# A hybrid decoder layer on one core: first loads in one queue, nine idle matmuls on ones, first products by token pairs, first sums in their own step, stores of row factors and states in longer runs

## The chip, the core and the metric

The kernel runs on one core of one Trainium2 chip. Its engines work beside each other, each through its own instructions in order: TensorE (PE) multiplies, VectorE (DVE), ScalarE (ACT) and GpSimd (POOL) work on tiles, and SyncE (SP) issues DMAs, as ACT and POOL also do. The metric is the device time of one execution in microseconds; lower is better.

## The reference

One inference step of one layer: 4096 prompt tokens and 64 sample tokens of width 1024 are normalised, multiplied by one large matrix, and the result is shared out among three head groups (a gated short convolution, windowed attention with sinks, attention to memory), whose outputs go through a second matrix.

```python
def _layer(x, conv_buf, buf_k, buf_v, mem_k, mem_v, g_pre, g_post, w_in, conv_w, sink, w_out, prompt):
    h = _rmsnorm(x, g_pre)
    z = h @ w_in
    cb, cc, ch, cg, q, k, v, ag, mq, mg = _split_cols(z)
    u = cc * ch
    up = jnp.concatenate([conv_buf, u], axis=1)
    conv = conv_w[0] * up[:, 0:t] + conv_w[1] * up[:, 1:t + 1] + conv_w[2] * up[:, 2:t + 2]
    out_a = jax.nn.silu(cg) * cb * conv
    ...
    y = jnp.concatenate([out_a, out_b, out_c], axis=-1) @ w_out
    return x + _rmsnorm(y, g_post), new_conv, new_k, new_v
```

Besides the two outputs, the last convolution inputs (`conv_prompt`, `conv_sample`), the new keys and values and the memory's keys and values are returned.

## The kernel before

**Tiles.** The 4160 tokens are cut into eight blocks (`NBLK`) of 520, each of two halves of 260 (`HW`). Tokens lie along the free dimension, the 1024 channels on 128 partitions by eight (`KT`). The input product z = h @ w_in is done in three phases, one per set of output columns (`PHASES`); phases 0 and 1 hold four pairs of 128 columns, q = 0 to 3, phase 2 three. A float32 product is made of three matmuls per 128 channels: value and weight are each split into a rounded part (`hi`) and the rest (`lo`), and hi x hi, hi x lo and lo x hi are added. ACT makes `hi` by a copy, DVE makes `lo` by a subtraction (`split` L383, `x_split` L608, `w_split` L214). One such product of 4 x 128 channels is 12 matmuls of 128x260 (`product` L392).

**Steps.** From block 2 of phase 0 on, each block takes seven steps p = 0 to 6 (`PRODUCTS`) of products with sums of quarter matrices in Winograd's way, instead of eight: of x the parts B11, B21, B12, B22 and the sums T1 = B12 - B11, T2 = B22 - T1, T3 = B22 - B12, T4 = B21 - T2 (`t_sum`, L367, DVE). Blocks 0 and 1 of phase 0 are done plainly in eight steps s = 0 to 7 (`plain_block` L697), since the sums of the weights (S1 to S4) aren't there yet. A step is four products, q = 0 to 3, 48 matmuls. The steps of the next block prepare its x: load, gain by channel (ACT), factor by token (DVE), T1, and the split of the step to come. With `high_first`, the eight matmuls with `hi` of x come ahead of the four with `lo`; before, this holds for q = 0 of steps 0 and 2 of phase 0 and for a few steps of phases 1 and 2 (`HIGH_FIRST`).

**Row factors.** 1 / rms of every token is computed from x in natural order: tiles `nat` of 104 tokens, five to a block, are squared and summed on ACT (`row_step` L300), POOL takes the power, and the 104x5 factors are stored to `rowd` in device memory (L321), from which they are loaded again, spread over all partitions (`rows_load` L282), when the block's x is scaled. `row_queue` (L341), called once in each step, counts the steps between store and load in `row_spreads`. For blocks 0 and 2 the factors also go through PE (`rows_diag`, `rows_product`).

**Order.** In phases 0 and 2 the five engines' instructions stand as the code is written (`written_order` L721); in phase 1 a scheduler places them, save those in `keep`. Each engine takes its own in order, so a wait holds what is behind it. SP issues nearly all loads in the same way; the stores of phase 0 go out from POOL (`store` L198).

**The start** (L726 to L745). The first half of x in two parts, and weight tiles of 128x512, `wr_qA21` for product q, are loaded: x and tiles 2, 3 from SP, tiles 0, 1 from ACT. Meanwhile PE works seven idle matmuls on `ones` and `ident`. The first step has the matmuls of a product in the order hi x hi for the four k, hi x lo for the four, lo x hi for the four (`opening`).

**Conv states.** `finish_conv` (L475) of block 0 stores the samples' last inputs from a tile of 8x10 (`o_convs`), that of the last block the prompt's (`o_convp`), both in phase 1.

Of the kernel before, what the change touches and what calls it, by code (L numbers as in the profile page):

```python
# [8 lines left out]
F32 = mybir.dt.float32  # L9
# [6 lines left out]
P = 128  # L16
# [36 lines left out]
def hybrid_layer(ctx: ExitStack, tc: tile.TileContext, a: dict):  # L53
# [31 lines left out]
    make_identity(nc, ident)  # L85
# [7 lines left out]
    zs = const.tile([P, 14, NS], F32, name="zs")  # L93

# [167 lines left out]
    def x_load(ph, b, o, parts=KH):  # L262
# [37 lines left out]
    def row_step():  # L300
# [13 lines left out]
        if i == 4:  # L314
            G.tensor_scalar(r[:RG, 0:5], r[:RG, 0:5], 1.0 / D, EPS, op0=ALU.mult, op1=ALU.add)
            G.tensor_tensor(r[:RG, 0:5], r[:RG, 0:5], mhalf[:RG, 0:5], op=ALU.pow)
# [4 lines left out]
            G.dma_start(rowd[b].rearrange("(i p) -> p i", p=RG), r[:RG, 0:5])  # L321
            if b > 0:
                row_spreads[b] = 4
# [17 lines left out]
    def row_queue():  # L341
# [4 lines left out]
        for b in [b for b, n in row_spreads.items() if n == 1]:  # L346
            rows_load(b)
# [44 lines left out]
    def product(w, h, bank, first=True, last=True, opening=False, high_first=False):  # L392
        order = [(l, r, k) for l, r in ((0, 0), (0, 1), (1, 0)) for k in range(KH)] if opening else \
# [68 lines left out]
    ub_prev, us_of = [None, None], []  # L462
# [12 lines left out]
    def finish_conv(b, ct, zc, zh, zg, zb):  # L475
# [6 lines left out]
        if ns:  # L482
# [4 lines left out]
            store(a["o_convs"][ct], us[:, :, 8:10])  # L487
# [5 lines left out]
        if b == NBLK - 1:  # L493
            store(a["o_convp"][ct], ub_prev[ct])
# [62 lines left out]
    def x_of(ph, b, o, parts=KH):  # L557
        if ph == 0 or b < PLAIN_BLOCKS:
            t = x_load(ph, b, o, parts)
# [17 lines left out]
    def next_block(ph, b, p):  # L577
# [19 lines left out]
        if nph < 2:  # L597
            if p == 6:
# [9 lines left out]
    def x_split(b, o):  # L608
        x = xs[0, b][o]
        h0[b, o] = hi, lo = [h_tile(n, f"{n}0_{b}{o}") for n in ("hi", "lo")]  # L610
        for k in range(KH):
# [40 lines left out]
    def plain_jobs(b, s):  # L652
# [16 lines left out]
            (0, 6): lambda: [*parts(1, "B11"), *row, *fills(1, "S1", "S4"), *sums(3, 0), *row],  # L669
            (0, 7): lambda: [*row, *fills(3, "S2", "S3"), lambda: rows_diag()],  # L670
# [65 lines left out]
    for _ in range(7):  # L736
        TE.matmul(idle[:, 0, :P], ones, ident, start=True, stop=True)
    w = ws[0, 0, "A21"] = w_slot(0, "w0_0A21")
    V.tensor_copy(w[:, 0], raw0[0, "A21"])
    x_split(0, "B11")  # L740
    V.tensor_tensor(w[:, 1], raw0.pop((0, "A21")), f(w[:, 0]), op=ALU.subtract)
# [251 lines left out]
    def input_projection():  # L993
        for i, (ph, b, p) in enumerate(steps):
# [66 lines left out]
            for q in quads:  # L1061
# [5 lines left out]
                product(ws[ph, q, PRODUCTS[p][0]], hs[i], acc[:, q % 2], high_first=q == 0 and (p in (0, 2) if ph == 0 else (ph, b, p) in HIGH_FIRST))  # L1067
# [10 lines left out]
            if p >= 5:  # L1078
# [4 lines left out]
                elif ph == 1 and b == 0:  # L1083
                    when = (1, *(2,) * len(ends))
# [804 lines left out]
```

## Time and profile before

| | us |
|---|---|
| median of 3 runs | 1456.57 |
| lowest and highest run | 1455.95, 1457.87 |
| the profiled execution | 1455.13 |
| its span in the trace | 1453.4 |
| start of the first product; of the second step | 5.77; 13.53 |
| start of step (2, 0) of phase 0 | 100.57 |
| start of block 1 of phase 1 | 380.45 |
| end of the last matmul | 1447.15 |

The profile is one execution, and all durations are from it. A row of a timeline has the start, the duration of the merged instructions, engine, line, operation, tiles (written <- read, without the buffers' numbers) and the count; in brackets stands how long the engine had been idle before, and who ended that. PE is busy in all stages, so where PE waits and how late it starts is what can be won; an idle time of another engine counts only where PE waits behind it. The page's chain of waits runs 82% of the span along PE, 8% along DMAs, 4% along DVE.

### The profile page before, as it was taken

To read this page: it belongs to the slowest core of one execution; us is meant where nothing else is said; L and a number is where in the kernel's file an instruction comes from. 1 tells how busy PE (TensorE), PEld (TensorE's weight loads), DVE (VectorE), ACT (ScalarE), POOL (GpSimd) and SP (SyncE) were. 2 spreads that over 40 slices of the span, in tenths; PEclk is the share of its full clock that TensorE was granted. 3 is DMA by queue.
4 is the path that set the end of the run, shared out by engine and by line. 5 is a ranking of instruction groups with operands and counts; after the bars stand their busy time and mean duration, and the time that the engine had idled before them with its cause. 6 is when DMAs were issued, how large, how long until landed. Compare 5 with 4: busy or idle time off the path is not lost.

```text
span 1453.4 us, 30932 instructions
## 1 busy us (share of the span) xinstructions
PE 1442.0 (99%) x11453; PEld 1324.3 (91%) x11453; DVE 1206.5 (83%) x1899; ACT 756.0 (52%) x1868; POOL 447.1 (31%) x622
## 2 busy tenths in 40 slices
PE   9999999999999999999999999999999999999998
PEld 9999999999999999999999999978777787777777
DVE  6879888899998877799678778998998889888853
ACT  6776665566522222234445534656566555655641
POOL 0223323212300000000002224275665566556661
PEclk9999999999999999999999999999999999999999
DMA  9999999896866644475987978999988899998773
GB/s 266 160 275 232 293 269 277 238 307 215 226 223 198 192 136 150 140 273 143 323 276 228 290 231 266 324 261 238 238 217 224 215 258 228 238 237 223 233 220 105
DMA packets 212124, 337.27 MB, mean 232 GB/s; under 512 B 55301, under 2 KB 126213, under 8 KB 211941
## 3 DMA queue, kind: packets, MB, share of 16 engines
q1 hardware_dynamic: 159189, 226.29, 52.7%
q0 software_dynamic: 44144, 78.68, 21.3%
q10 hardware_dynamic: 8640, 30.33, 6.7%
q8 instruction: 91, 1.49, 0.5%
q14 instruction: 60, 0.49, 0.1%
HBM read 192.48 MB, written 110.15 MB: 208 GB/s over the span
## 4 chain that ended last, share of the span: by engine, by line
PE 82%; DMA 8%; DVE 4%; issue 3%; ACT 2%; SPq 1%; POOL 1%; POOLq 0%; ACTq 0%; DVEq 0%
PE c L397 46%; PE y L1675 24%; PE pv L1144 5%; PE ws L1144 3%; DMA place<-in_xt 2%; PE xs L1144 2%; DMA nat<-in_x_p 2%; DMA wr_3A<-in_w_in 1%; PE mem_acc L825 1%; DMA md<-th 1%; DVE z L649 1%; DMA x_1B<-in_xt 1%; DMA vd<-v 1%; DMA wr_3S<-sd6S 1%; DMA w<-s 0%
## 5 line engine op out<-in xcount | busy, mean ns | idle before, releaser
L1675 PE MATMUL y<-wo,mh 128*128 128x512 f32 (+1 forms) x1040 | 328.7, 391 | 0.0
L403 DVE TENSOR_TENSOR z<-c,z 128x520 f32<-128x520 f32 (+1 forms) x308 | 193.6, 644 | 61.3 <-PE c L397 60.5
L1675 PEld LDWEIGHTS y<-wo,mh 128*128 128x128 f32 x1040 | 194.2, 188 | 52.4 <-DVE wmx L1303 5.4
L1675 PE MATMUL y<-wo,ml 128*128 128x512 f32 (+1 forms) x520 | 201.0, 387 | 0.0
L1347 POOL TENSOR_SCALAR s<-s,x 128x256 f32<-128x256 f32 x124 | 58.0, 480 | 199.1 <-DVE x L1342 193.5
L1675 PEld LDWEIGHTS y<-wo,ml 128*128 128x128 f32 x520 | 97.8, 188 | 18.5
L1313 ACT ACTIVATE s<-s,wnm 128x128 f32<-128x128 f32 x256 | 98.7, 387 | 0.0
L771 POOL MEMSET negs<- 128x1 f32 x1 | 0.1, 100 | 281.7 <-DVE w_2A L219 281.7
L1290 ACT COPY s<-ws 128x256 f32<-128x256 f32 x128 | 41.3, 378 | 77.4 <-PE ws L1144 68.5
L1705 POOL TENSOR_TENSOR xr<-yn,xr 128x1024 f32<-128x1024 f32 x29 | 69.3, 2390 | 18.4 <-ACT yn L1704 17.7
L1378 POOL TENSOR_SCALAR_AFFINE_SELECT wd<-w 128x512 f32<-128x512 f32 x64 | 60.2, 941 | 38.2 <-DMA w<-s 21.7
L1683 ACT ACTIVATE y<-y 128x512 f32<-128x512 f32 (+1 forms) x66 | 38.6, 585 | 52.8 <-DVE yn L1682 52.7
L1336 ACT ACTIVATE s<-xs,x 128x256 f32<-128x256 f32 x128 | 58.1, 461 | 0.0
L1682 DVE TENSOR_TENSOR yn<-y,gpost 128x512 f32<-128x512 f32 (+1 forms) x66 | 44.7, 677 | 16.0 <-PE y L1675 14.5
L1144 PEld LDWEIGHTS ws<-kst,q 64*128 64x128 f32 x768 | 47.7, 185 | 11.0 <-issue 9.5
L1378 POOL TENSOR_SCALAR_AFFINE_SELECT w<-w 128x512 f32<-128x512 f32 x64 | 55.5, 887 | 2.2
L1144 PE MATMUL ws<-kst,q 64*128 64x256 f32 x768 | 55.0, 288 | 0.0
L1294 DVE COPY_PREDICATED s<-wmask,ws 128x256 f32<-128x256 uint8 x124 | 48.0, 441 | 8.0 <-ACT s L1290 6.0
L309 ACT ACTIVATE nat<-nat 104x1024 f32<-104x1024 f32 x40 | 42.3, 1058 | 19.2 <-DMA nat<-in_x_p 19.2
L405 ACT COPY z<-c 128x520 f32<-128x520 f32 (+1 forms) x44 | 24.1, 553 | 53.0 <-PE c L397 50.0
L1313 ACT ACTIVATION_READ_ACCUMULATOR s<-s,wnm 128x1 f32 x256 | 47.9, 187 | 0.0
L200 POOL DMA_DIRECT2D md<-th x48 | 26.2, 547 | 66.9 <-DVE th L457 40.3
(970 smaller groups left out, 4805.6 us busy)
## 6 DMA issues: line engine op xcount, KB each, us to landing
w<-s SPq DMA_DIRECT2D x456, 64.0 KB
q<-qd POOLq DMA_DIRECT2D x32, 768.0 KB, 6.6
xr<-in_x_p SPq DMA_DIRECT2D x32, 512.0 KB
nat<-in_x_p SPq DMA_DIRECT2D x39, 416.0 KB
o_yp<-xr SPq DMA_DIRECT2D x31, 512.0 KB
md<-th POOLq DMA_DIRECT2D x48, 260.0 KB, 7.0
qd<-zh SPq DMA_DIRECT2D x48, 260.0 KB
qd<-z SPq DMA_DIRECT2D x48, 260.0 KB
```

What stands on the lines that cost most here:

```text
L309: S.activation(t[:RG], t[:RG], AF.Square, accum_out=r[:RG, i : i + 1])
L397: TE.matmul(bank[:, :HW], w[:, l, k * P : (k + 1) * P], h[r][:, k], start=first and i == 0, stop=last and i == 3 * KH - 1)
L403: add = lambda dst, other: V.tensor_tensor(dst, c, other, op=ALU.add)
L1144: ins = TE.matmul(o, w, x, **kw)
L1294: V.copy_predicated(to, squares(third["wmask"]), squares(s3[:, :, 0:P]))
L1313: S.activation(sm[:, h], sm[:, h], AF.Exp, bias=nm[:, h : h + 1], scale=SCALE, accum_out=den[:, h : h + 1])
L1336: S.activation(p[:, i], s[:, i].rearrange("p (a k j) -> p a k j", a=2, k=4), AF.Exp, bias=nm[:, i : i + 1], scale=SCALE, accum_out=den[:, ...
L1347: G.tensor_scalar(p[:, i], p[:, i], rd[:, i : i + 1], 0.5, op0=ALU.mult, op1=ALU.mult)
L1378: G.affine_select(out, src, pattern=[[32 * sign, 2], [0, 8], [sign, 32]], compare_op=op, fill=0.0, base=base * sign, channel_multiplier=-s ...
L1675: TE.matmul(acc, self.hl[l][:, k], wo[k][c0 // 512][:, r, c0 % 512 : c0 % 512 + c1 - c0], start=j == 0, stop=j == passes * KT - 1)
L1682: V.tensor_tensor(yn[:m, c0:c1], acc[:m], gpost[0][:m, c0:c1], op=ALU.mult)
L1705: total = G.tensor_tensor(self.xr, yn, self.xr, op=ALU.add)
```

## The change

The first loads all go out from SP, x's second part after weight tile 0 (`between`), and weight tile 0 is split like the others, its `hi` now by ACT. The nine idle matmuls use `ones` twice, and `ones` is filled before `ident`. `opening` goes by pairs of k. The row factors are turned on DVE (a 32x32 transpose of `turned`, a part of `zs`), so that the store writes runs of 32 or 8 floats instead of single ones, two `row_queue` calls later than before; `rows_diag` comes a step earlier. T1 of a block is summed in the block's own step 0, ahead of T2 in the list of jobs there, not in step 6 of the block before. `high_first` holds for q = 0 of every step of phase 0. In phase 1 the splits of steps 0 and 1 of block 0 are kept in place, and block 0's second conv finish moves from two steps later to three. `o_convs` is packed by POOL ahead of its store, and `o_convp` is stored in phase 2.

```diff
     ones = const.tile([P, P], F32, name="ones")
     G.memset(ones, 1.0)
+    make_identity(nc, ident)
...
+    turned = zs[:, 10, 0:32]
+    G.memset(turned, 0.0)
...
             for k in range(0, KH, parts):
+                if k:
+                    between()
                 DMA.dma_start(t[:, k : k + parts, g - g0 : g - g0 + w], src[:, KH * kh + k : KH * kh + k + parts, off : off + w])
...
-            G.dma_start(rowd[b].rearrange("(i p) -> p i", p=RG), r[:RG, 0:5])
-            if b > 0:
-                row_spreads[b] = 4
+            G.tensor_copy(turned[:RG, 0:5], r[:RG, 0:5])
+            row_spreads[b] = 4
...
-        for b in [b for b, n in row_spreads.items() if n == 1]:
+        for b in [b for b, n in row_spreads.items() if n == 3]:
+            V.transpose(turned, turned)
+            for g in range(0, RG, 32):
+                n = min(32, RG - g)
+                G.dma_start(rowd[b].rearrange("(i p) -> i p", p=RG)[:, g : g + n], turned[g : g + 5, :n])
+        for b in [b for b, n in row_spreads.items() if n == 1 and b > 0]:
             rows_load(b)
...
-        order = [(l, r, k) for l, r in ((0, 0), (0, 1), (1, 0)) for k in range(KH)] if opening else \
+        order = [(l, r, k + n) for k in (0, 2) for l, r, n in ((0, 0, 0), (0, 1, 0), (0, 0, 1), (1, 0, 0), (0, 1, 1), (1, 0, 1))] if opening else \
...
-            store(a["o_convs"][ct], us[:, :, 8:10])
+            last = tiny.tile([P, 16], F32, tag="x4", name=f"convs{ct}")
+            G.tensor_copy(last.rearrange("p (b t) -> p b t", b=NB), us[:, :, 8:10])
+            store(a["o_convs"][ct].rearrange("p b t -> p (b t)"), last)
...
-            store(a["o_convp"][ct], ub_prev[ct])
+            convp.append(lambda: store(a["o_convp"][ct], ub_prev[ct]))
...
-            hs[i] = split(xs[ph, b][o], f"{ph}_{b}{o}", (ph, b) == (1, 1) and p < 2)
+            hs[i] = split(xs[ph, b][o], f"{ph}_{b}{o}", (ph, b) in ((1, 0), (1, 1)) and p < 2)
...
-            if p == 6:
+            if (nph, nb, p) == (1, 0, 6):
                 jobs.append(lambda: t_sum(nph, nb, "T1"))
...
-            (0, 6): lambda: [*parts(1, "B11"), *row, *fills(1, "S1", "S4"), *sums(3, 0), *row],
-            (0, 7): lambda: [*row, *fills(3, "S2", "S3"), lambda: rows_diag()],
+            (0, 6): lambda: [*parts(1, "B11"), lambda: rows_diag(), *row, *fills(1, "S1", "S4"), *sums(3, 0), *row],
+            (0, 7): lambda: [*row, *fills(3, "S2", "S3")],
...
-    x_of(0, 0, "B11", 2)
-    first_w("A21", 0, queue=S)
     S.mul(tiny.tile([P, 16], F32, tag="x4", name="table")[:, :8], mhalf, 1.0)
-    first_w("A21", 1, queue=S)
-    first_w("A21", 2, 3)
+    x_of(0, 0, "B11", 2, lambda: first_w("A21", 0))
+    first_w("A21", 1, 2, 3)
...
-    for _ in range(7):
-        TE.matmul(idle[:, 0, :P], ones, ident, start=True, stop=True)
-    w = ws[0, 0, "A21"] = w_slot(0, "w0_0A21")
-    V.tensor_copy(w[:, 0], raw0[0, "A21"])
-    x_split(0, "B11")
-    V.tensor_tensor(w[:, 1], raw0.pop((0, "A21")), f(w[:, 0]), op=ALU.subtract)
+    for _ in range(9):
+        TE.matmul(idle[:, 0, :P], ones, ones, start=True, stop=True)
+    x_split(0, "B11", 0)
+    first_fill("A21", 0)
+    x_split(0, "B11", 1, 2, 3)
...
+            if ph < 2 and p == 0 and i and (ph, b) != (1, 0):
+                jobs.insert(0, lambda: t_sum(ph, b, "T1"))
...
+            if (ph, b, p) == (2, 3, 0):
+                jobs += convp
...
-                product(ws[ph, q, PRODUCTS[p][0]], hs[i], acc[:, q % 2], high_first=q == 0 and (p in (0, 2) if ph == 0 else (ph, b, p) in HIGH_FIRST))
+                product(ws[ph, q, PRODUCTS[p][0]], hs[i], acc[:, q % 2], high_first=q == 0 and (ph == 0 or (ph, b, p) in HIGH_FIRST))
...
-                    when = (1, *(2,) * len(ends))
+                    when = (1, *(p - 3,) * len(ends))
```

Where this moves instructions is read from the order on each engine. First SP at the start of the program, before; `x_0B` is the first part of x, `wr_qA` the weight tile of product q:

```order
L271 DMA x_0B_214<-in_xt 128x2x260 x2
L225 DMA wr_2A_223<-in_w_in 128x512
L225 DMA wr_3A_225<-in_w_in 128x512
L225 DMA wr_0A_227<-in_w_in 128x512
L225 DMA wr_1A_229<-in_w_in 128x512
L271 DMA x_0B_231<-in_xt 128x4x260
```

SP at the same place with the change:

```order
L275 DMA x_0B_217<-in_xt 128x2x260
L227 DMA wr_0A_219<-in_w_in 128x512
L275 DMA x_0B_217<-in_xt 128x2x260
L227 DMA wr_1A_222<-in_w_in 128x512
L227 DMA wr_2A_224<-in_w_in 128x512
L227 DMA wr_3A_226<-in_w_in 128x512
L227 DMA wr_0A_228<-in_w_in 128x512
L227 DMA wr_1A_230<-in_w_in 128x512
L275 DMA x_0B_232<-in_xt 128x4x260
```

Tiles 0 and 1, which ACT loaded before, now stand in SP's list, tile 0 between the two parts of x. Next DVE around step 0 of block 1 of phase 1, before; `x_1T` are the sums T1 and T2, `lo_1B` and `lo_1T` the split parts for PE, `place` in the last sum is T3, `cacc` and `ub` belong to the convolution:

```order
L376 TENSOR_TENSOR x_1T_5124<-place,x_1B_4692 128x1040
L386 TENSOR_TENSOR lo_1B_5129<-x_1B_4900,hi_1B_5128 128x1040
L376 TENSOR_TENSOR x_1T_5146<-place,x_1T_5124 128x1040
L473 SCALAR_TENSOR_TENSOR z_0_2_0_4733<-cth_1_5161,z_0_2_0_4733 128x520
...
L376 TENSOR_TENSOR place<-place 128x1040
L507 SCALAR_TENSOR_TENSOR cacc_0_5185<-ub_0_5179,convw,cacc_0_5185 128x456
L403 TENSOR_TENSOR z_1_2_0_5246<-c_1_2_1_5247,z_1_2_1_5164 128x2x260
L508 TENSOR_TENSOR cacc_0_5185<-cacc_0_5185,z_0_0_0_4702 128x456
L480 SCALAR_TENSOR_TENSOR z_0_2_0_4733<-z_0_2_1_4663,z_0_2_0_4733 128x520
L484 MEMSET ub_1_5274 128x2
L490 TENSOR_TENSOR ub_1_5274<-z_0_2_0_4733,z_0_2_1_4663 128x456
L386 TENSOR_TENSOR lo_1T_5295<-place,hi_1T_5294 128x1040
```

DVE at the same place with the change:

```order
L394 TENSOR_TENSOR lo_1B_5164<-x_1B_4938,hi_1B_5163 128x1040
L384 TENSOR_TENSOR x_1T_5181<-place,x_1B_4730 128x1040
L481 SCALAR_TENSOR_TENSOR z_0_2_0_4771<-cth_1_5212,z_0_2_0_4771 128x520
L384 TENSOR_TENSOR x_1T_5196<-place,x_1T_5181 128x1040
...
L488 SCALAR_TENSOR_TENSOR z_0_2_0_4771<-z_0_2_1_4701,z_0_2_0_4771 128x520
...
L518 TENSOR_TENSOR cacc_0_5237<-cacc_0_5237,z_0_0_0_4740 128x456
L384 TENSOR_TENSOR place<-place 128x1040
L492 MEMSET ub_1_5359 128x2
L500 TENSOR_TENSOR ub_1_5359<-z_0_2_0_4771,z_0_2_1_4701 128x456
L411 TENSOR_TENSOR z_1_0_0_5258<-c_1_0_2_5318,z_1_0_1_5167 128x2x260
L394 TENSOR_TENSOR lo_1T_5315<-place,hi_1T_5314 128x1040
```

The split `lo_1B` stands ahead of the sum T1; the sum T3 comes behind the conv work that it preceded, and one more addition from PE's accumulators stands ahead of its split. In phase 0 the same happens with T1, here block 3, before:

```order
L363 TENSOR_TENSOR place<-place,rb_1755 128x1040
L376 TENSOR_TENSOR x_3T_2003<-place,x_3B_1574 128x1040
L386 TENSOR_TENSOR lo_3B_2006<-x_3B_1770,hi_3B_2005 128x1040
L376 TENSOR_TENSOR x_3T_2023<-place,x_3T_2003 128x1040
L457 SCALAR_TENSOR_TENSOR th_6_2038<-th_6_2038,z_2_2_0_1616 128x520
```

and with the change:

```order
L371 TENSOR_TENSOR place<-place,rb_1773 128x1040
L394 TENSOR_TENSOR lo_3B_2022<-x_3B_1788,hi_3B_2021 128x1040
L384 TENSOR_TENSOR x_3T_2039<-place,x_3B_1587 128x1040
L384 TENSOR_TENSOR x_3T_2041<-place,x_3T_2039 128x1040
L465 SCALAR_TENSOR_TENSOR th_6_2056<-th_6_2056,z_2_2_0_1629 128x520
```

The split for step 1 moves ahead of the sum T1; nothing else changes there. In blocks 0 to 2 of phase 0, T1's place is as before.

More of the change, by code (lines that the diff above doesn't have):

```diff
@@ L84, in hybrid_layer @@
     ident = const.tile([P, P], F32, name="ident")
-    make_identity(nc, ident)
     ones = const.tile([P, P], F32, name="ones")
     G.memset(ones, 1.0)
+    make_identity(nc, ident)
     mhalf = const.tile([P, 8], F32, name="mhalf")
@@ L260, in x_tile, with x_load @@
         return place[:, kept.index(o)] if o in kept else hxp.tile([P, KH, HW], F32, tag="hx", name=f"x{ph}_{b}{o}")
-    def x_load(ph, b, o, parts=KH):
+    def x_load(ph, b, o, parts=KH, between=lambda: None):
         kh, g0 = int(o[1]) - 1, (2 * b + int(o[2]) - 1) * HW
@@ L460, in finish_gate @@
         store(md[idx, :, tokens(b)], th)
-    ub_prev, us_of = [None, None], []
+    ub_prev, us_of, convp = [None, None], [], []
     def us_load():
@@ L553, in h_split, with x_of @@
             o = PRODUCTS[p][1]
-            hs[i] = split(xs[ph, b][o], f"{ph}_{b}{o}", (ph, b) == (1, 1) and p < 2)
-    def x_of(ph, b, o, parts=KH):
+            hs[i] = split(xs[ph, b][o], f"{ph}_{b}{o}", (ph, b) in ((1, 0), (1, 1)) and p < 2)
+    def x_of(ph, b, o, *parts):
         if ph == 0 or b < PLAIN_BLOCKS:
-            t = x_load(ph, b, o, parts)
+            t = x_load(ph, b, o, *parts)
         else:
@@ L606, in hybrid_layer, with x_split @@
     raw0, zz, pending, h0, kept = {}, {}, {}, {}, {}
-    def x_split(b, o):
+    def x_split(b, o, *ks):
         x = xs[0, b][o]
-        h0[b, o] = hi, lo = [h_tile(n, f"{n}0_{b}{o}") for n in ("hi", "lo")]
-        for k in range(KH):
+        hi, lo = h0[b, o] = h0.get((b, o)) or [h_tile(n, f"{n}0_{b}{o}") for n in ("hi", "lo")]
+        for k in ks or range(KH):
             g = gain_of(o, k)
```

## The prediction

> **What bounds the kernel now.** I read the page's busy table first, then who waited for whom on PE, then the order of time around each wait, then the DMA rate stage by stage.
>
> ```profile
> PE 1442.0 (99%) x11453; PEld 1324.3 (91%) x11453; DVE 1206.5 (83%) x1899; ACT 756.0 (52%) x1868; POOL 447.1 (31%) x622
> ...
> PE idle L737 <- POOL mhalf L89: 1.5, 1, 1.5
> PE c L397 <- DVE lo_1T L386: 1.0, 1, 1.0
> PE c L397 <- DVE w_0A L739: 0.9, 1, 0.9
> PE c L397 <- DVE lo_1B L386: 0.7, 1, 0.7
> ...
> PE c L397 <- DVE lo_6B L386: 0.3, 1, 0.3
> PE c L397 <- DVE lo_2T L386: 0.2, 1, 0.2
> ```
>
> PE is busy all but 11.4 us, and all its waits together are 4.9 us (columns: total, times, longest). So the change cannot touch the bulk: it can win the slow start, and the waits for `lo` tiles. The start, PE's rows in order of time (start, us, instruction, count):
>
> ```profile
> 1.54 3.35 PE L737 MATMUL idle<-ident,ones 128*128 128x128 f32 x14 [1.54 <-POOL mhalf L89]
> 5.77 1.54 PE L397 MATMUL c<-hi_0B,w_0A 128*128 128x260 f32 x4 [0.88 <-DVE w_0A L739]
> ...
> 8.91 0.99 PE L397 MATMUL c<-hi_0B,w_1A 128*128 128x260 f32 x4
> 9.74 0.64 PE L397 MATMUL c<-lo_0B,w_1A 128*128 128x260 f32 x4
> 10.22 0.64 PE L397 MATMUL c<-hi_0B,w_1A 128*128 128x260 f32 x4
> ...
> 13.53 0.28 PE L397 MATMUL c<-lo_0B,w_0A 128*128 128x260 f32 x1
> ```
>
> From 9.74 to 10.22 four products take 0.48 us, 0.119 each; from 8.91 to 9.74 they take 0.83, 0.21 each. So PE reaches its full pace only at about 9.7 us, although the clock column reads 1.00 in every stage. The first 48 products end at 13.53; at full pace they need 48 x 0.119 = 5.7 us.
>
> **Term 1, the start.** What PE waits for there is the arrival of data, then ACT and DVE (start, us):
>
> ```profile
> 4.01 0.91 ACT L613 ACTIVATE hi_0B<-x_0B,gpre 128x260 fp32r<-128x260 f32 x2 [0.77 <-DMA x_0B<-in_xt]
> 5.20 0.43 DVE L739 CAST w_0A<-wr_0A 128x512 fp32r<-128x512 f32 x1 [5.20 <-DMA wr_0A<-in_w_in]
> 5.54 1.68 DVE L614 SCALAR_TENSOR_TENSOR lo_0B<-x_0B,gpre,hi_0B 128x260 fp32r<-128x260 f32 x4
> 7.23 0.62 ACT L215 CAST w_1A<-wr_1A 128x512 fp32r<-128x512 f32 x1 [0.55 <-DMA wr_1A<-in_w_in]
> 7.88 0.69 DVE L219 TENSOR_TENSOR w_1A<-wr_1A,w_1A 128x512 fp32r<-128x512 f32 x1
> ...
> 2.00:3.00 1.00, 1.00 (x7) 1.00 0.90 228
> 3.00:4.00 1.00, 1.00 (x6) 1.00 1.08 300
> 4.00:5.00 1.00, 0.89 (x5) 1.00 0.95 300
> 5.00:6.00 1.00, 0.23 (x1) 1.00 1.05 364
> 6.00:7.00 1.00, 1.00 (x4) 1.00 1.02 313
> 7.00:8.00 1.00, 1.00 (x6) 1.00 1.02 373
> ```
>
> The last number of a stage row is GB/s. By it 228, 528, 828, 1192, 1505 and 1878 KB have moved at 3, 4, 5, 6, 7 and 8 us. Now two queues mix the tiles, and weight tile 0, second by need, lands at 5.20. In one queue the order is: half of x (266 KB), weight 0 (262), other half, weights 1, 2, 3. At the same rate the bytes are there at 3.1, 4.0, 4.9, 5.6, 6.4 and 7.2. Landing is seen later: the first half of x at 4.01, 0.9 after 266 KB. I take 0.6 (bounds 0.3 and 1.2), so weight 0 lands at 4.6. Then ACT casts it (0.62) to 5.2 and makes the other three `hi` (some 0.43 each) to 6.45; DVE's `lo` of the last quarter ends at 6.9. By token pairs the first product ends at 7.1. Weight 1 is cast to 7.0, its `lo` (0.69) is there at 7.7, where the fourth matmul of product two wants it; nine more give 8.8. Weights 2 and 3 have their `lo` at 8.3 and 9.1, ahead of PE: 1.42 us a product, so 10.2 and 11.6. Against 13.53 that is **-1.9 us**; with weight 0 at 4.3 or 5.2 it is -2.2 or -1.3.
>
> That needs PE at full pace from about 7. The `ones` are now filled first, so the idle matmuls can start near 1.1, and nine at 3.35/7 us end at 5.4: PE is busy without the 0.88 us gap. Before, the full pace came 3.9 us after the gap. If it came 3.9 us after 5.4, product one would end at 8.2, 17 matmuls would be done by 9.3, and the rest at 13.0: -0.5. I take **-1.8**.
> The Trainium skill, TensorE: Matmul & The Clock Gate, Part 1, says that PE gets its full rate after one busy window of about 3.4 us, and that the windows run free of the kernel. By that rule alone, an estimate from that page, the full pace comes between 4.5 and 7.9, and the term is -1.9 to -1.3. The trace agrees so far: 3.9 us of unbroken products until 9.7.
>
> What could hide it: the steps behind must be fed 1.8 us earlier too. The tightest feed is DVE's at 100 to 118 us, and behind that the DMAs:
>
> ```profile
> 42.23 1.18 POOL L321 DMA_DIRECT2D rowd<-r  x1 [0.31 <-POOL r L316]
> 54.90 1.01 POOL L321 DMA_DIRECT2D rowd<-r  x1 [0.31 <-POOL r L316]
> ...
> 49.00:56.00 7.00, 7.00 (x61) 1.00 1.02 91
> 62.00:71.00 9.00, 9.00 (x78) 1.00 0.87 77
> 71.00:76.00 5.00, 5.00 (x45) 1.00 1.05 301
> ...
> 262.00:268.00 6.00, 5.70 (x48) 1.00 1.08 96
> 385.00:396.00 11.00, 10.29 (x86) 10.08 (x86) 11.00 (x16) 2.44 (x3) 10.06 (x10) 1.00 1.06 82
> ...
> DMA to landing us min/median/max: 8.7/11.5/14.5
> ```
>
> Seven us after each of these stores of row factors (520 elements of 4 bytes; the last line is of all seven such stores) the rate is 91 and 77 GB/s for seven and nine us, where 301 is usual, with the DMA engines booked full. It is so in block 6 (96), and from 385 (82), behind the two `o_convs` stores of 1024 elements of 8 bytes; that row has all engines: PE, PE's loads, DVE, ACT, POOL. The change writes 20 runs of 32 or 128 bytes, and rows of 64 bytes. I take it that the stall goes: then loads and stores between 49 and 80 land several us earlier, and the lead lasts. Its cost: seven DVE transposes of 128x32, none dearer than the 0.69 of a 128x512 tile, 4.8 us in all on an engine with 17% of its time free; three more POOL issues a store of at most 1.18, on an engine 69% idle; and `rows_diag` a step earlier, ahead of DVE's work for later products. These lie beside PE's work; if one stood in front of a late `lo`, it would cost up to 0.7. The `convs` copy and the later `convp` stores lie on POOL and SP, and no wait of PE names those: nothing, or as much as one of those copies (0.7) at worst.
> The Trainium skill, DMA: Bandwidth & Descriptors, Specifications, says that writes below 512 bytes are done as read-modify-write. By that rule the new runs stay slow, though 20 stand for 520; no run here shows which counts. That result is the first rival.
>
> **Terms 2 and 3, `lo` before T1, and high parts first.** PE at the four waits, and two rows of DVE, the T1 sum that stands before `lo_6B` and the last `lo`:
>
> ```profile
> 117.59 0.40 PE L397 MATMUL c<-hi_2T,w_3S 128*128 128x260 f32 x2
> 118.22 0.36 PE L397 MATMUL c<-lo_2T,w_0S 128*128 128x260 f32 x1 [0.23 <-DVE lo_2T L386]
> 266.51 0.36 PE L397 MATMUL c<-lo_6B,w_0A 128*128 128x260 f32 x1 [0.30 <-DVE lo_6B L386]
> 386.13 1.11 PE L397 MATMUL c<-hi_1B,w_0A 128*128 128x260 f32 x8
> 387.96 0.75 PE L397 MATMUL c<-lo_1B,w_0A 128*128 128x260 f32 x4 [0.71 <-DVE lo_1B L386]
> 399.65 0.36 PE L397 MATMUL c<-lo_1T,w_0S 128*128 128x260 f32 x1 [1.00 <-DVE lo_1T L386]
> ...
> 263.98 1.24 DVE L376 TENSOR_TENSOR x_6T<-place,x_6B 128x1040 f32<-128x1040 f32 x1
> 398.14 1.36 DVE L386 TENSOR_TENSOR lo_1T<-place,hi_1T 128x1040 fp32r<-128x1040 f32 x1
> ```
>
> From 117.59 two matmuls should take 0.24 and the next starts 0.63 later: 0.4 lost; 266.51 is the like, 0.45. With eight `hi` products first, `lo` is wanted 8 x 0.119 = 0.95 us later, and in blocks 3 to 7 it also stands one 128x1040 sum (1.24) earlier on DVE. Both waits go: **-0.85**. The order costs PE nothing, as the same products are made.
>
> **Term 4, block 1 of phase 1.** At 387.96 PE is 0.9 late (386.13 + 0.95 = 387.08); the `lo` now stands ahead of the T1 sum, so this goes. But DVE works without a pause there (11.00 of 11.00 us from 385 to 396), and the `lo` of T3, 398.14 to 399.5, closes it. By the new order the T3 sum and its `lo` still follow the same conv work, and one more accumulation (`c_1_0_2`, 128x520, about the 0.69 of a 128x512 tile) stands in front. So PE, 0.9 early, waits 0.9 longer: it resumes at 399.65 or up to 0.7 later, all less the lead, as this chain follows PE's own end of phase 0. **0** (bounds -1.9, both waits gone: 0.9 and 1.0, and +0.7).
>
> Sum: -1.8 - 0.85 + 0 = -2.65 on the profiled execution (1455.13, span 1453.4 and 1.7 around it): 1452.5. That execution is 1.44 below the median of the runs (1456.57). The start is the part that can differ from run to run, and the change shortens it; I add half, 0.7: **1453.2**.
>
> **Rivals.**
> (A) The stores still stall the DMAs. Then the chain into DVE's `lo` just before 118.22 stays, PE can pass there at most 0.95 earlier, and with 0.45 at block 6 the sum is -1.4: 1453.7, plus 0.7 is 1454.4. For it: the new runs are still far under the size of the kernel's other rows. Against: 26 times fewer pieces.
> (B) The lead is not kept into phase 1, that is, the change doesn't do what it says: loads there come at their old time, DVE's `lo` ends at 399.5 as before, and PE resumes at 399.65. Nothing is gained: 1455.1, plus 0.7, 1455.8. For it: PE waits longest there, and DVE has no slack. Against: these loads wait for buffers that the end of phase 0 frees.
> (C) Term 4 comes in full, as DVE's chain is shorter there than I count: -1.9 more, 1451.3.
> (D) Slower: SP's load of the row factors now stands two steps (2 x 48 x 0.119 = 11.4 us) behind their store, before four. If the store still lands after 14.5 us, SP stands 3.1 us in each of blocks 3 to 7 with the next loads behind it. Of that the high parts cover 0.95; five blocks lose 2.15 each, 10.8: 1464.0. It decides from a landing of 12.3 us on; without the stall I expect under 8.
>
> **How the numbers follow.** Forecast 0.58, A 0.16, B 0.12, C 0.09, D 0.05. The forecast's own range is 1452.1 (term 1 at -2.2, none of the 0.7) to 1455.2 (term 1 at -0.5, term 4 at +0.7). For 8 in 10 I reach to 1450.2, C with term 1 at -2.2 and none of the 0.7, and to 1455.8, B. A measurement tells 0.2% from no change, so faster is under 1453.7: six tenths of the forecast, all of C and a third of A, 0.50; slower is D, 0.05; the same 0.45.
>
> **What would show it.** Start: first real product near 5.4, 48 done by 11.6, no slow matmuls after 8. Stores: rates above 200 GB/s at 49 to 71 and at 262 to 268. Waits: no `lo_2T`, `lo_6B`, `lo_1B` in PE's list; one `lo_1T` wait of about 2 us in phase 1. I am wrong if the lead at 100 us is under 1 us, if it is gone at 400 us, or if SP waits on `rowd`.

## The result and the profile after

| | before | with the change |
|---|---|---|
| median of 6 runs, us | 1456.38 | 1467.36 |
| lowest and highest | 1455.93, 1458.54 | 1463.39, 1470.34 |
| the profiled execution | 1455.13 | 1466.47 |
| its span | 1453.4 | 1464.8 |

The ratio is 1.0071, with an interval of 1.0055 to 1.0087: the changed kernel is slower by 11 us, where 1453.2 was forecast and 1455.8 was the upper end of the range. The page's busy table of the changed kernel looks as before:

```profile
PE 1445.4 (99%) x11457; PEld 1326.3 (91%) x11457; DVE 1211.0 (83%) x1905; ACT 756.0 (52%) x1869; POOL 461.2 (31%) x653
```

PE's busy time has grown by 3.4 us. The four instructions more are idle matmuls (18 for 14), 0.9 us by 4.21/18 each; so other matmuls must have become slower. Who is waited for on PE (columns: total, times, longest) says where to look:

```profile
PE ws L1155 <- DMA q<-qd: 7.5, 1, 7.5
PE c L405 <- DVE lo_1T L394: 2.3, 2, 2.1
PE pv L1155 <- ACT y L1694: 1.4, 3, 0.9
PE idle L745 <- POOL ones L86: 1.1, 1, 1.1
```

The waits that the change was to remove (`w_0A`, `lo_2T`, `lo_6B`, `lo_1B`) are gone. In their place stands one of 7.5 us that was on no list before, for a load named `q`. PE's rows in order of time, at the places at which the prediction measured:

```profile
1.06 4.21 PE L745 MATMUL idle<-ones 128*128 128x128 f32 x18 [1.06 <-POOL ones L86]
5.26 0.39 PE L405 MATMUL c<-hi_0B,w_0A 128*128 128x260 f32 x1
...
7.67 0.28 PE L405 MATMUL c<-hi_0B,w_0A 128*128 128x260 f32 x1
7.79 0.28 PE L405 MATMUL c<-hi_0B,w_1A 128*128 128x260 f32 x1
...
12.23 0.28 PE L405 MATMUL c<-lo_0B,w_0A 128*128 128x260 f32 x1
...
99.26 0.52 PE L405 MATMUL c<-hi_2B,w_0A 128*128 128x260 f32 x3
...
378.10 0.87 PE L405 MATMUL c<-hi_1B,w_0A 128*128 128x260 f32 x5
...
395.89 0.40 PE L405 MATMUL c<-hi_1T,w_3S 128*128 128x260 f32 x2
398.36 0.36 PE L405 MATMUL c<-lo_1T,w_0S 128*128 128x260 f32 x1 [2.07 <-DVE lo_1T L394]
...
971.90 0.38 PE L1155 MATMUL ws<-kst,q 64*128 64x256 f32 x2
979.80 2.72 PE L1155 MATMUL ws<-kst,q 64*128 64x256 f32 x22 [7.51 <-DMA q<-qd]
982.31 1.49 PE L1155 MATMUL xs<-mk,q 64*128 64x256 f32 x12
...
1458.13 0.28 PE L1686 MATMUL y<-wo,mh 128*128 128x256 f32 x1
```

and PE's rows of before at the same place of the output stage:

```profile
972.61 1.69 PE L1144 MATMUL ws<-kst,q 64*128 64x256 f32 x24
974.14 0.88 PE L1144 MATMUL xs<-mk,q 64*128 64x256 f32 x12
```

Against before, PE is 1.3 us early at the second step (12.23 against 13.53) and at step (2, 0) (99.26 against 100.57), 2.35 early at block 1 of phase 1 (378.10 against 380.45), 1.29 early behind `lo_1T` (398.36 against 399.65), and still 0.7 early at 972 (971.90 against 972.61). Then all is lost at one place. The 24 `ws` and 12 `xs` matmuls, which took 2.41 us (972.61 to 975.02), take 11.90 (971.90 to 983.80). Of the 9.5 us lost, 7.5 are the wait; the rest is the clock, as 22 `ws` now take 2.72 us where 24 took 1.69. The stages of the changed kernel (PE, PE's loads, DVE, ACT, POOL; granted clock, DMA share, GB/s):

```profile
4.00:5.00 1.00, 1.00 (x6) 0.97 (x5) 0.49 (x1) 0.63 (x2) 0.00 (x0) 1.00 0.66 194
49.00:56.00 7.00, 7.00 (x61) 7.00 (x60) 5.93 (x10) 5.91 (x12) 2.14 (x4) 1.00 0.94 225
62.00:71.00 9.00, 9.00 (x78) 9.00 (x77) 8.83 (x19) 8.97 (x20) 5.24 (x10) 1.00 0.86 275
262.00:268.00 6.00, 6.00 (x53) 6.00 (x52) 5.96 (x9) 4.85 (x9) 2.98 (x6) 1.00 0.83 279
385.00:396.00 11.00, 10.75 (x91) 10.55 (x90) 11.00 (x18) 1.24 (x3) 10.27 (x11) 1.00 0.63 218
399.00:402.00 3.00, 3.00 (x28) 3.00 (x27) 3.00 (x6) 0.00 (x0) 0.00 (x0) 1.00 1.03 376
972.00:980.00 8.00, 0.49 (x4) 0.29 (x6) 0.76 (x2) 0.00 (x0) 1.43 (x2) 0.66 1.12 290
980.00:985.00 5.00, 5.00 (x48) 4.78 (x50) 2.98 (x6) 3.04 (x7) 1.76 (x3) 0.52 0.44 112
```

From 980 to 985 the granted clock is 0.52. Behind that, the gap to before grows from 8.8 us (983.80 against 975.02) to 11.3 at the last matmul (1458.41 against 1447.15), in small waits spread over the stage, such as the 1.4 for `y`.

**What this place is.** In the output stage the 4096 prompt tokens pass in chunks of 256. For each, POOL loads the queries `q` in two halves of 768 KB (L1193) and SP loads, for even chunks, the 1 MB of gated products into `place` (L1201). At 964 us POOL issues the second half of `q` of chunk 3 and SP at about the same time the `place` of chunk 2. POOL's DMAs before (start, us; the bracket gives idle time ahead; "issue" is a wait for nothing that the profile shows):

```profile
929.11 0.90 POOL L1190 DMA_DIRECT2D mix<-md  x1 [3.82 <-issue]
...
964.33 0.57 POOL L1696 TENSOR_TENSOR yst<-yst,mhalf 128x1 f32<-128x1 f32 x1
964.87 0.89 POOL L1182 DMA_DIRECT2D q<-qd  x1
```

POOL with the change:

```profile
925.72 0.90 POOL L1201 DMA_DIRECT2D mix<-md  x1 [1.43 <-PE c L405]
...
963.59 0.58 POOL L1707 TENSOR_TENSOR yst<-yst,mhalf 128x1 f32<-128x1 f32 x1
965.46 0.90 POOL L1193 DMA_DIRECT2D q<-qd  x1 [1.29 <-issue]
```

and SP, before and with the change:

```profile
965.79 0.45 SPq L1190 DMA_DIRECT2D place<-md  x1
```

```profile
965.04 0.59 SPq L1201 DMA_DIRECT2D place<-md  x1
```

A stall with no cause in sight stood at 925 us before, ahead of a load that nobody was short of, and stands at 964 us now, ahead of `q`. Before, `q` was issued 0.92 us ahead of `place`; now it is issued 0.42 behind it. The order of the instructions in the stage is the same in both kernels. What the DMA engines did from 965 to 970 us (queue, packets, MB, share; q0 is POOL's queue, q1 SP's), before:

```profile
q0 software_dynamic: 844, 0.89, 74.8%
q1 hardware_dynamic: 437, 0.40, 30.6%
```

and with the change:

```profile
q1 hardware_dynamic: 1200, 1.18, 85.5%
q0 software_dynamic: 14, 0.00, 0.5%
```

Once SP's megabyte is ahead, POOL's queue moves 14 packets in 5 us. `q` lands 14.3 us after its issue, near 979.8, where it took 5.9 before and landed near 970.8, some 1.8 us ahead of the first `ws`. The Trainium skill, DMA: Bandwidth & Descriptors, section on queues, rings and completion order, has each DMA engine take turns between the queues that have work for it, packet by packet. By that rule, an estimate, about half of the 1214 packets would be POOL's; these rows disagree. From 971 to 974 us, with both queues at work, the same trace has 270 packets of POOL's queue and 264 of SP's, as the rule says. Why the queue that comes second moves next to nothing at first stays open.

### The profile page after: what moved, and what is told of

The parts are those of the page before. It is cut to its first block, busy times and chain, and to the rows that moved or that the text cites. A ratio compares the mean times of both kernels' runs of the same rounds, so it can differ in the third digit from the quotient of the medians.

```text
span 1464.8 us, 30985 instructions
## 1 busy us (share of the span) xinstructions
PE 1445.4 (99%) x11457; PEld 1326.3 (91%) x11457; DVE 1211.0 (83%) x1905; ACT 756.0 (52%) x1869; POOL 461.2 (31%) x653
## 4 chain that ended last, share of the span: by engine, by line
PE 82%; DMA 6%; issue 3%; SPq 3%; DVE 3%; POOL 1%; ACT 1%; ACTq 0%; POOLq 0%; DVEq 0%
PE c L405 54%; PE y L1686 19%; PE pv L1155 4%; SPq L1373 2%; PE ws L1155 2%; DMA mix<-md 1%; DMA w<-s 1%; DMA q<-qd 1%; PE xs L1155 1%; PE mem_acc L832 1%; DMA wr_3S<-sd6S 1%; DMA place<-md 1%; DMA vd<-v 0%; DMA x_1B<-in_xt 0%; DMA xr<-in_x_p 0%
## 5 line engine op out<-in xcount | busy, mean ns | idle before, releaser
L1693 DVE TENSOR_TENSOR yn<-y,gpost 128x512 f32<-128x512 f32 (+1 forms) x66 | 44.6, 676 | 14.3 <-PE y L1686 13.2
L1715 ACT ACTIVATE yn<-yn,yst 128x1024 f32<-128x1024 f32 x29 | 33.3, 1150 | 21.5 <-POOL yst L1707 21.5
L1340 DVE TENSOR_REDUCE x<-xs 128x2 f32<-128x512 f32 x64 | 43.7, 682 | 0.0
```

The lines of the kernel that those rows point to most:

```text
L1340: V.tensor_reduce(mx, s, axis=AX.X, op=ALU.max)
L1693: V.tensor_tensor(yn[:m, c0:c1], acc[:m], gpost[0][:m, c0:c1], op=ALU.mult)
```

## The experiments

Each ran beside the kernel before on the same chip. There were three chips, and the kernel before had medians of 1455.79 to 1456.58 there; differences to the changed kernel (1467.36) are taken across them. Times are medians in us; the ratio is to the kernel before.

| run | n | median | before | ratio, interval |
|---|---|---|---|---|
| a_mix_late | 10 | 1461.13 | 1456.53 | 1.0028, 1.0018 to 1.0038 |
| b_start | 10 | 1455.63 | 1456.53 | 0.9994, 0.9985 to 1.0003 |
| b_stores | 4 | 1464.32 | 1456.53 | 1.0050, 1.0033 to 1.0068 |
| b_order | 10 | 1457.37 | 1456.53 | 1.0012, 1.0001 to 1.0023 |
| a_pad60 | 4 | 1464.43 | 1456.58 | 1.0058, 1.0043 to 1.0073 |
| a_pad60_mix | 5 | 1460.64 | 1456.58 | 1.0036, 1.0018 to 1.0054 |
| b_pad33 | 10 | 1455.63 | 1456.58 | 0.9993, 0.9983 to 1.0004 |
| a_no_stores | 10 | 1457.75 | 1456.58 | 1.0009, 1.0000 to 1.0018 |
| b_late_q | 4 | 1467.66 | 1456.56 | 1.0081, 1.0055 to 1.0106 |
| a_desc | 10 | 1454.94 | 1456.56 | 0.9986, 0.9974 to 0.9998 |
| a_q_sp | 10 | 1458.13 | 1456.56 | 1.0015, 1.0004 to 1.0026 |
| a_q_sp_conv | 10 | 1453.65 | 1456.56 | 0.9979, 0.9967 to 0.9990 |
| b_late_q2 | 4 | 1462.00 | 1455.79 | 1.0045, 1.0030 to 1.0060 |
| b_spare | 5 | 1460.56 | 1455.79 | 1.0033, 1.0015 to 1.0051 |

### First: which part of the change, and is it the race of the two loads?

**a_mix_late**: the changed kernel, with SP's `place` load of chunk 2 a few products later, out of `q`'s way.

```diff
-            at(0, 0, lambda: chunks[2].load_mix())
...
+        if i == 2:
+            at(0, 5, lambda: chunks[2].load_mix())
```

> The changed kernel with one load moved: in block 2 of the output stage SP issues the load of place (1 MB) behind the two loads and stores that follow it, not ahead of them; nothing else differs. Theory Q (the loss is one wait of 7.5 us and the half clock behind it, since place stands ahead of the q load of POOL in the DMA engines, where it stood behind it before): the q load lands about 6 us after its issue instead of 14.3, PE doesn't wait at 972 us, and the time falls by 9 to 11 us to 1455 to 1457. Rival S (the loss has another cause, of which the wait is a sign only, such as slower loads in all of the output stage): the wait moves to another load and the time stays above 1462.

The median falls by 6.2 us against the changed kernel, a little over half of the loss; it lies between the two theories' ranges. In its profile POOL still stalls 1.29 ahead of `q`, but `q` lands 8.0 us after issue and PE waits 1.4. That profiled execution (1455.77) is the lowest of the ten, so the median run loses more than it shows; with `place` out of the way, the next load of SP's list, 0.5 MB of `xr`, is issued at 964.24, ahead of `q` at 964.58.

**b_start**, **b_stores**, **b_order**: the kernel before with one third of the change each. b_start has the loads, idle matmuls and `opening` of the start; b_stores the row factors turned, `rows_diag` earlier, and the `convs` and `convp` stores; b_order T1, `high_first`, the kept splits and the later conv finish.

```diff
+    x_of(0, 0, "B11", 2, lambda: first_w("A21", 0))
+    first_w("A21", 1, 2, 3)
...
+    for _ in range(9):
+        TE.matmul(idle[:, 0, :P], ones, ones, start=True, stop=True)
```

> The kernel before with the start alone: one queue, nine idle matmuls, products by token pairs. POOL's program has the same instructions as before, save that ones is filled first. Theory T (a shift in time by 1 us is enough to turn the order of the q load and the place load round): the q load waits and the time is 1463 or more. Theory P (POOL comes late to the q load because its own program is longer, by the stores): q lands in 6 us as before and the lead of 1.3 us stays, 1455.0 to 1455.5.

The time doesn't differ from before: the lead of the start, which theory P kept, is lost. In the profiled execution, 1.2 us above the median, it goes at 60 us: the row factors are ready 3.8 us later than before (their store starts at 58.72, before at 54.90), and the product with them waits behind `rows_diag`, which stands at its old place:

```profile
60.11 1.11 PE L339 MATMUL rows_y<-mix_s,ones 104*128 104x260 f32 x4 [3.30 <-DVE mix_s L330]
```

Why they are later is not shown.

```diff
+            G.tensor_copy(turned[:RG, 0:5], r[:RG, 0:5])
...
+            V.transpose(turned, turned)
...
+                G.dma_start(rowd[b].rearrange("(i p) -> i p", p=RG)[:, g : g + n], turned[g : g + 5, :n])
```

> The kernel before with the stores alone: row factors turned and stored in runs, o_convs packed, o_convp stored later. PE's order is that of before. Theory T: there is no lead at 965 us, so the loads keep their order and the time is 1455.5 to 1457. Theory P: POOL issues q over 1 us later against SP's place load, PE waits some 7 us, and the time is 1464 or more.

The stores alone cost 7.8 us, and the loss is the same one: in its profile POOL stalls ahead of `q`, and PE waits for it behind SP's `place` of 965.75.

```profile
966.29 0.90 POOL L1192 DMA_DIRECT2D q<-qd  x1 [1.29 <-issue]
...
977.94 2.71 PE L1154 MATMUL ws<-kst,q 64*128 64x256 f32 x22 [4.86 <-DMA q<-qd]
```

```diff
+            if ph < 2 and p == 0 and i and (ph, b) != (1, 0):
+                jobs.insert(0, lambda: t_sum(ph, b, "T1"))
...
+                product(ws[ph, q, PRODUCTS[p][0]], hs[i], acc[:, q % 2], high_first=q == 0 and (ph == 0 or (ph, b, p) in HIGH_FIRST))
...
+                    when = (1, *(p - 3,) * len(ends))
```

> The kernel before with the order alone: T1 in its own step, the products with the high parts first in all steps of phase 0, the edits of phase 1. The three waits for lo in phase 0 go, worth 1.1 us by the changed kernel's trace, and the wait in block 1 of phase 1 grows by 1.1, so PE is where it was at 420 us. Theory T and theory P both give 1455.5 to 1457.5 with q landing in 6 us; a time above 1462 would speak for neither and say that the edits of phase 1 do it.

No gain, 0.8 us more if anything; its wait for `lo_1T` is 1.7 us where before has 1.0. So the stores are the part that loses, at a place some 700 us behind the last store of row factors. The three parts (-0.9, +7.8, +0.8) don't add up to 11: how much the race costs depends on how the two loads fall.

### Second: what moves POOL's stall?

Two theories were left. The changed kernel has more POOL instructions ahead of `q` (a stall that comes after so many instructions), or POOL's DMAs write other numbers of descriptors (a stall that comes after so many of those: a store of 520 single elements is now 20 runs).

**a_pad60**: the changed kernel and 60 more instructions on POOL; **a_pad60_mix** the same with the `place` load late, as in a_mix_late; **b_pad33**: the kernel before and 33.

```diff
+    for _ in range(60):
+        G.memset(turned[:, 31:32], 0.0)
```

> The changed kernel with 60 memsets of one column more on POOL at its start, where it is idle until 39 us; DMAs and all other engines as they are. In the three kernels with the new stores POOL stands 1.29 us with nothing to wait for at the same place of its program (its 528th instruction, the q load behind yst at 964 us). Theory I (the stall belongs to a place in POOL's instructions, counted from the start): it moves 60 instructions ahead, POOL issues q without it, before place, and the time falls to 1453 to 1458. Theory R (the stall belongs to the DMA descriptors that POOL has written, which the memsets don't change): q stalls 1.29 us at the same load and the time stays at 1463 to 1470.

> The same 60 memsets, and the load of place behind the other loads of its block, as in the run with that alone (1461.1 median, 1455.8 to 1463.5). Theory I: both causes gone, 1452 to 1455 with a smaller spread. Theory R: as with the moved load alone, 1459 to 1463.

> The kernel before with 33 memsets of one column on POOL at its start, and nothing else: as many as the changed kernel has instructions more ahead of the q load. Theory I: the stall of 1.29 us stands at that q load as in the changed kernel, place goes ahead of it, and the time is 1461 or more, by memsets that nothing waits for. Theory R: 1455.5 to 1458, as before.

The stall stands where it stood, in a_pad60's row of POOL:

```profile
963.96 0.90 POOL L1195 DMA_DIRECT2D q<-qd  x1 [1.43 <-issue]
```

b_pad33 shows none there and takes the time of before. The number of instructions is out. a_pad60_mix repeats a_mix_late (1460.64 against 1461.13): the loss is halved, and its profile has a wait for `q` of 4.6.

**a_no_stores**: the changed kernel with the stores of before.

```diff
-            G.tensor_copy(turned[:RG, 0:5], r[:RG, 0:5])
+            G.dma_start(rowd[b].rearrange("(i p) -> p i", p=RG), r[:RG, 0:5])
...
-            convp.append(lambda: store(a["o_convp"][ct], ub_prev[ct]))
+            store(a["o_convp"][ct], ub_prev[ct])
```

> The changed kernel with the old stores of row factors, o_convs and o_convp; the start and the order stay. POOL's program is as long as before, so by both theories the stall is not at the q load and q lands ahead of place. The lead is the start's 1.3 us and what the order wins while the old stores hold the DMAs up (0 to 1.1): 1454.0 to 1456.0. A time above 1461 would take the loss from the stores.

No wait for `q`, and 9.6 us less than the changed kernel. But it isn't faster than before, as it should be by the loss at `q` alone (1454.0 to 1456.0 was expected): by difference, a second cost of about 2 us sits in the rest of the change.

**a_desc** tests the descriptors: the changed kernel, and in phase 2 three useless copies from POOL, of 1024, 1024 and 768 pieces of 256 bytes.

```diff
+                for c, n in ((0, 8), (1, 8), (2, 6)):
+                    jobs.append(lambda c=c, n=n: G.dma_start(spare[c, :, :n, :64], a["x_p"][P * c : P * c + P].rearrange("p (a n) -> p a n", a=8)[:, :n, :64]))
```

> The changed kernel with three copies of input x to unused device memory on POOL's queue in phase 2 (at 765 us), 2816 pieces of 256 bytes, which nothing waits for. Theory R (POOL's stall of 1.3 us belongs to the count of descriptors that it has written): 2816 more move the stall to the mix load at 925 us, where it stood before the change (3.8 us of idle time there); q goes out 1.3 us earlier at 964 us and ahead of place, PE's long wait goes, 1454 to 1459. If the stall belongs to the count of DMAs or to something else, it stays at q, and the time at 1463 to 1468.

With more work than the changed kernel, it is 12.4 us faster. POOL's stall is back at the `mix` load, and `q` goes ahead of SP's `place` of 963.93 and lands after 6.3 us:

```profile
925.61 0.90 POOL L1204 DMA_DIRECT2D mix<-md  x1 [3.45 <-issue]
...
963.28 0.90 POOL L1196 DMA_DIRECT2D q<-qd  x1
```

So POOL's own copies move the stall. That it goes by the number of their pieces (descriptors) is inferred, as the other counts don't fit. A mark at a number of POOL's DMAs would have come earlier in the changed kernel, which has 21 more of them ahead (28 stores of row factors where 7 were); the stall came 19 DMAs later. The bytes of those stores are the same in both, so a mark in bytes would have stayed. Fewer pieces went with a later stall, 2816 more with an earlier one. At which count of pieces it comes, and what stands behind it, stays open.

**b_late_q**, **b_late_q2**, **b_spare**: is a late `q` enough? The kernel before, with eight small instructions on POOL ahead of `q`, into a new tile in b_late_q, into one that is there in b_late_q2 (whose edit this is). b_spare has the new tile of 128x8 alone.

```diff
+                for _ in range(8):
+                    G.memset(mhalf[:, 7:8], -0.5)
                 chunks[3].load_queries(1)
```

> The kernel before with eight memsets (about 1.25 us together) on POOL right ahead of the second half of the q load of chunk 3, and nothing else. Theory Q (the order of the q load on POOL and the place load on SP is what costs the time): q goes out behind place, lands 11 to 14 us after its issue instead of 5.9, PE waits 4 to 8 us at 973 us, half clock follows, and the time is 1462 to 1467, for 1.25 us of work on an engine that is idle half of the time. Rival S (the loss has another cause): 1456 to 1458.

> As b_late_q, the kernel before with eight memsets on POOL ahead of the q load, but on a column of mhalf that is there already, so that no tile is added. Theory Q: q behind place, PE waits 4 to 8 us at 973 us with half clock behind it, matmuls at 118.44 ns, 1460 to 1465. Rival S: 1456 to 1458, and b_late_q was slow by its pace alone.

> The kernel before with the tile of 128x8 alone (one memset at the start, nothing reads it). If its 32 bytes, by which all tiles behind it move, slow the matmuls down: 119.1 ns from one to the next in the input product and 1460 to 1464. If the slow pace was that chip's or that hour's: 118.44 ns and 1455.5 to 1457.5.

b_late_q, at 1467.66 above the range of both theories, has the turned order and a PE wait of 4.6, but its matmuls are slower everywhere, so it can't be read by itself. b_late_q2 is clean:

```profile
964.67 1.18 POOL L1248 MEMSET mhalf<- 128x1 f32 x8
966.00 0.89 POOL L1182 DMA_DIRECT2D q<-qd  x1
...
977.23 2.71 PE L1144 MATMUL ws<-kst,q 64*128 64x256 f32 x22 [4.74 <-DMA q<-qd]
```

SP's `place` is issued at 965.63 there. So 1.2 us of work on an engine that is 69% idle costs 6.2 us, with none of the change. b_spare explains the other: 32 bytes a partition ahead of the other tiles cost 4.8 us, at the full granted clock. PE from 430 to 530 us, before, then b_spare, then b_late_q2 beside b_spare on the same chip:

```profile
430.00:530.00 100.00, 100.00 (x847) 100.00 (x846) 84.49 (x118) 22.59 (x25) 0.00 (x0) 1.00 0.65 204
```

```profile
430.00:530.00 100.00, 100.00 (x842) 100.00 (x841) 85.26 (x121) 24.15 (x27) 0.00 (x0) 1.00 0.64 203
```

```profile
430.00:530.00 100.00, 100.00 (x847) 100.00 (x847) 84.03 (x117) 22.59 (x25) 0.00 (x0) 1.00 0.64 200
```

842 matmuls where there were 847: 0.6%, on an engine that never waits there. b_late_q, on another chip, also has 842, so the pace goes with the tile and not with the chip.

### Third: the second cost, and a version without both

**a_q_sp**: the changed kernel, with that half of `q` loaded by SP, ahead of SP's other loads, and with `place` late, as in a_mix_late. **a_q_sp_conv**: the same, and block 0's second conv finish two steps later, as before, not three.

```diff
+            at(0, 0, lambda: chunks[3].load_queries(1, DMA))
...
-                    when = (1, *(p - 3,) * len(ends))
+                    when = (1, *(p - 2,) * len(ends))
```

(The last two lines are a_q_sp_conv's alone.)

> The changed kernel with the second half of the q load of chunk 3 issued by SP ahead of its other loads, not by POOL, and the place load of that block behind the others. Theory Q: q goes out at 964 us whatever POOL does and lands by 971; no wait on q at 972, so the lead of 1.3 us that PE has at 420 us is kept: 1454 to 1456.5; the spread of single runs beyond that comes from half clock after the 2 us wait in phase 1. Rival S: over 1461.

> The same, and the second conv finish of block 0 of phase 1 four steps later instead of three, so that DVE has 4 us less to do ahead of the lo of T3. The wait of 2.1 us at 399 us goes, and with it the half clock that some runs have behind it: 1452 to 1454, and a smaller spread than without it. If the time is the same as without it, that wait was no loss.

Neither waits for `q`. a_q_sp is 9.2 us faster than the changed kernel and still slower than before, above the 1454 to 1456.5 that was expected; a_q_sp_conv is 4.5 us faster again, and the one run that is clearly faster than before: 0.9979, the interval ends at 0.9990 (a_desc's at 0.9998). The gap between their two profiles grows from 0.3 to 4.1 us between 396 and 406 us, and 3.4 are left at the end. PE in a_q_sp there:

```profile
398.49 0.36 PE L405 MATMUL c<-lo_1T,w_0S 128*128 128x260 f32 x1 [2.06 <-DVE lo_1T L394]
398.69 0.55 PE L405 MATMUL c<-hi_1T,w_0S 128*128 128x260 f32 x2
```

and its stage:

```profile
399.00:402.00 3.00, 3.00 (x16) 3.00 (x15) 3.00 (x6) 0.00 (x0) 0.00 (x0) 0.50 1.01 371
```

16 matmuls, where the changed kernel makes 28 in the same 3 us (its row stands above): after a wait of 2.06 us the granted clock is 0.50 for some 3.4 us. In a_q_sp_conv there is no wait for `lo_1T` at all. The Trainium skill, TensorE: Matmul & The Clock Gate, section on why this matters for kernels, wants no gaps of more than about 3 us between matmuls; by that 2.06 us would be harmless, and b_start's 3.30 at 60 us would not. The runs bear out neither. The profiles with waits of 2.04 to 2.07 us split: half clock behind it in a_q_sp and a_pad60_mix, none in the changed kernel and a_mix_late. Behind the wait in b_start the granted clock stays at 1.00:

```profile
61.00:64.00 3.00, 3.00 (x27) 2.97 (x26) 1.58 (x4) 2.32 (x5) 0.00 (x0) 1.00 0.94 236
```

Behind waits of 1.7 and less (b_order, a_pad60, a_no_stores, a_desc) none has half clock; behind all of the waits for `q` of 4.6 to 7.5 us it comes. The wait itself also differs between executions: a_desc has the same later conv finish and waits 0.9 for `lo_1T`, and on a_q_sp's chip its median is 3.2 us lower than a_q_sp's. What shortens it there is not shown.

## Why the prediction was wrong, point by point

- **Term 1, -1.8.** Right in kind, 0.5 too large: -1.3. The idle matmuls ran from 1.06 and the first product began at 5.26, as said (1.1 and 5.4); the full pace came from 7.7 us on, with no slow matmul after 8, as said. The first product ended near 7.8 and not at 7.1, as the second half of x landed later than the even rate gave: 194 GB/s from 4 to 5 us, where 300 was taken. Up to there PE follows the data: the last three `lo` products start at 6.38, 7.03 and 7.50, each just behind its tile. ACT's last `hi` and DVE's last `lo` of the first step, on which it waits:

```profile
5.94 0.92 ACT L623 ACTIVATE hi_0B<-x_0B,gpre 128x260 fp32r<-128x260 f32 x2 [0.32 <-DMA x_0B<-in_xt]
6.49 0.90 DVE L624 SCALAR_TENSOR_TENSOR lo_0B<-x_0B,gpre,hi_0B 128x260 fp32r<-128x260 f32 x2 [0.16 <-ACT hi_0B L623]
```

  The last `lo` ends at 7.39, not at 6.9.
- **The stall of the DMAs behind the stores goes.** Right: 225, 275, 279 and 218 GB/s in the stages that had 91, 77, 96 and 82, and the stores land sooner (minimum, median, maximum over all of them):

```profile
DMA to landing us min/median/max: 3.9/4.9/7.3
```

  So rival A was wrong. But one of the prediction's own signs of being wrong is there: SP waits on `rowd`, five times.

```profile
SPq L288 <- DMA rowd<-zs: 32.1, 5, 9.0
```

  The prediction put SP's load 11.4 us behind the store. In fact SP comes to it at 148.96 in one block, 0.7 us behind POOL's first store there (148.25), and issues it at 154.69. The price that rival D put on this did not come: before, the same load went out at 154.26, and PE's list has no wait between the first products and 390 us.
- **Terms 2 and 3, -0.85.** Right: -1.04 (from -1.31 to -2.35), and the three waits are gone. Alone, without the stores, b_order shows no gain in the time.
- **Term 4, 0.** Outside its bounds: +1.06. The two waits became one of 2.07 us, as said, and 1.3 us of lead were left behind it. Neither rival B (no lead left) nor C (both waits gone) came. What I didn't see is that a wait of that length can be followed by half clock. a_q_sp with a_q_sp_conv shows that the later conv finish makes the wait, and that it costs 4.5 us in the median there, with `q` out of the way.
- **The step that failed** is the cost of the stores: "three more POOL issues a store of at most 1.18, on an engine 69% idle", of which the prediction said "These lie beside PE's work". That counted POOL's time where the stores stand. It did not ask what else the stores set on POOL, and no part of the prediction looked at the output stage. There `q` landed some 1.8 us before it was needed, with a megabyte of SP's issued 0.92 us behind it. The stores took the stall of POOL from 925 to 964 us, and with it this place: -1.3 at 399 us became +11.3 at the end. b_stores shows that the stores do it, a_desc that moving the stall away from `q` takes the loss away, b_late_q2 that 1.2 us of delay are enough. No rival had this mechanism, and slower had a chance of 0.05.
- **What the forecast got right shows once that is gone, in part:** a_desc, the whole change with `q` ahead again, gains 1.6 us on the kernel before beside it (1454.94 against 1456.56), where 3.4 were forecast. a_q_sp_conv comes to 1453.65, near the forecast of 1453.2, but it takes back the later conv finish, so it is not the kernel that was forecast.

The row that would have warned was in the trace of before: `mix<-md` with 3.82 us of idle time and nothing that it waited for.

Open stay: what sets the place at which POOL stalls; how the 2.5 us behind the half clock, at 985 to 1458, divide; and, in a_no_stores, how much of its 1457.75 is the wait at 399 us, since its profiled execution (1455.14) is the lowest of the ten and shows 1.6 us at the full clock.

## What to carry to other kernels

An edit of POOL's DMAs is not priced where it stands alone: look in the whole trace for DMAs of POOL that idle with no releaser, and for each load on the path how long before its use it lands and which large load of another queue is issued just behind it. A load that is short of slack belongs in the same queue as its rival, ahead of it, where the order is written and not raced for. And a wait of PE of 2 us or more may cost twice, by the clock behind it, so two short waits may be better than one that is as long as both; the waits of 2.06 and 3.30 us here show that its length alone doesn't say whether.

## What was not expected of the hardware

- POOL's queue got 14 of 1214 packets in 5 us beside a load of 1 MB from SP's queue that was 0.42 us ahead; issued 0.92 us earlier than that load, it got 844 of 1281. With both under way, from 971 to 974 us, the two got 270 and 264.
- POOL stalls at a DMA for 1.3 us and more with nothing to wait for; 2816 additional pieces moved the place, 60 additional instructions did not.
- PE's granted clock was 0.50 for some 3.4 us after a wait of 2.06 us, in two of four profiles with such a wait, and 1.00 after a wait of 3.30 us in a fifth.
- A tile of 32 bytes a partition ahead of the others slowed the matmuls by 0.6% at a granted clock of 1.00. It did so on two chips. That it is the addresses of the tiles was only argued.
